# The reciprocal square roots of a hybrid backbone's norms: one power instruction on GpSimd in place of Newton steps on VectorE

## The chip, the core and the metric

The kernel runs on one core of a Trainium2 chip. The metric is the device time of one execution in microseconds (us). Before the change three runs gave 3520.69, 3523.40 and 3524.45 us, a median of 3523.4 us. A lower time is better.

## What is computed

Two layers of a diffusion backbone over 9 tiles of 128 tokens (8 latent, 1 context), 1024 features. Each layer norms, mixes and norms again; the mixers are grouped-query attention (GQA), low-rank attention (MLA) and a state-space part, with shared projections in and out and a squared-ReLU MLP behind.

```python
def rmsnorm(x, g):
    xf = x.astype(F32)
    y = xf * lax.rsqrt(jnp.mean(xf * xf, axis=-1, keepdims=True) + EPS)
    return (y * g.astype(F32)).astype(x.dtype)

def trunk_layer(x, mod, p, ctx):
    shift1, scale1, gate1, shift2, scale2, gate2 = jnp.split(mod[:, None, :].astype(x.dtype), 6, axis=-1)
    h = rmsnorm(x, p['norm_mix_pre']) * (1 + scale1) + shift1
    mix, ctx_tensors = token_mixers(h, p, ctx)
    x = x + gate1 * rmsnorm(mix, p['norm_mix_post'])
    h = rmsnorm(x, p['norm_ffn_pre']) * (1 + scale2) + shift2
    f = jnp.square(jax.nn.relu(h @ p['w_ffn1'])) @ p['w_ffn2']
    x = x + gate2 * rmsnorm(f, p['norm_ffn_post'])
    return x, ctx_tensors
```

Inside `token_mixers` there are more norms of the same kind: of each head of the queries and keys of GQA, of the compressed queries and keys of MLA, and of the output of the state-space part.

## The kernel before, in words

Tokens go in three blocks (b) of three tiles of 128. Every product is made of two float32r halves, high and low, so each weight is loaded (`raw`), its high half cast on ScalarE (line 65) and its low half subtracted on GpSimd (line 78, tile `w`, five buffers). GpSimd has this as its main work; it also does some adds of squares (`h`, `big`), rotary products (`rope_a`, `rope_b`) and parts of the state-space scan.

A layer goes through these stages: the in-projection (in the first layer up to about 395 us, in the second from about 1880 to 2140 us), the two attentions with the state-space outputs beside them (to 700 and 2440 us), the out-projection and the norms around it (to 960 and 2680 us), and the MLP in eight chunks, the last of which goes block by block with the closing norms beside it.

Every norm needs 1/sqrt of a few columns, made by `rsqrt` (lines 99 to 117) on VectorE: a first guess from the bits (`rs_i`, `rs_h`, `rs_r`, line 89), then three Newton steps of a product (line 83), a product (line 83) and a fused step (line 93). That is 12 instructions, or 9 where there is one column. It is called from four places:

- `stats` (line 274), three columns, 24 times: the norms over 1024 features. TensorE sums the squares (`st`), VectorE adds EPS (`st_v`), `rsqrt` follows, VectorE spreads the result over a diagonal, and TensorE broadcasts that (`rb`).
- `in_proj`, group 2 (line 632), two columns, 18 times: compressed queries and keys of MLA. ScalarE (`qcn`) and VectorE (`ckv`) scale the projection by it.
- `in_proj`, group 1 (line 664), eight columns, 18 times: heads of GQA. The tile's squares are summed on VectorE (`vv`, line 662), `rsqrt` follows, VectorE multiplies the projection `g` by it into `g_qn`, and the rotation follows on GpSimd and VectorE.
- `ssm_b` (line 1311), one column, 18 times: the state-space output (`yss`, `y`).

The order of instructions on each engine is not the order of the code. Work beside the main stream is issued by `pull`, which pays it against a credit that `spend` counts (lines 57 to 61); the Newton instructions go through `ts`, `tt` and `stt` and are counted there. Then the framework's scheduler orders each engine's instructions. The engines take their own in that order.

Of the kernel before, what the change touches and what calls it, by code (L numbers as in the profile page):

```python
# [13 lines left out]
L = 2  # L14
NT = 9            # token tiles: 8 latent, 1 context
NB = 3            # blocks of three token tiles
BK = 384
EPS = 1e-6
# how long (ns) background work is left alone where a chain over several engines is under way
# [3 lines left out]
# worth (ns) of background work issued at each point of the main stream  # L23
PU = (600, 850, 600, 500, 1100, 500, 400, 400, 500, 900)
SEG = [[(0, 384, 0)], [(0, 384, 0)], [(0, 256, 0), (256, 384, 1)]]
# columns of the packed small parameters
# [4 lines left out]
class Group:  # L31
    """One head of one block of queries in the attention stream."""
# [5 lines left out]
class Net:  # L38
# [7 lines left out]
    # ---------------------------------------------------------------- helpers  # L46
# [9 lines left out]
    # Rough prices (ns) of what is issued, so that background work can be paced.  # L56
# [42 lines left out]
    def rsqrt(self, v, n):  # L99
        """1/sqrt of v [128, n], by Newton's steps in float32."""  # L100
        sp, nc = self.sp, self.nc
        ii = sp.tile([128, 16], I32, name="rs_i", bufs=2)[:, :n]
        r = sp.tile([128, 16], F32, name="rs_r", bufs=4)[:, :n]
        h = sp.tile([128, 16], F32, name="rs_h", bufs=2)[:, :n]
        t = sp.tile([128, 16], F32, name="rs_t", bufs=2)[:, :n]
        self.ts(ii, v.bitcast(I32), 1, ALU.arith_shift_right)
        self.ts(r.bitcast(I32), ii, -1.0, ALU.mult, float(0x5F3759DF), ALU.add)
        self.ts(h, v, -0.5, ALU.mult)
        for _ in range(3):
            if n == 1:  # L110
                self.ts(t, r, r, ALU.mult, h, ALU.mult)
                self.ts(r, t, 1.5, ALU.add, r, ALU.mult)
            else:
                self.tt(t, r, r, ALU.mult)
                self.tt(t, t, h, ALU.mult)
                self.stt(r, t, 1.5, r, ALU.add, ALU.mult)
        return r
# [12 lines left out]
    # Work that runs beside the main stream: generators, advanced a step at a time.  # L130
    # One that yields a number is left alone for about so many ns.
# [7 lines left out]
    def turns(self, gens):  # L139
        """Advances the generators in the list in turn; more may be added to it meanwhile."""  # L140
        due = {}
        while gens:
            ready = [g for g in gens if due.get(g, 0) <= self.now]
            if not ready:
                g = min(gens, key=lambda g: due[g])
                yield due[g] - self.now
                ready = [g]
            for g in ready:
                try:
                    due[g] = self.now + (next(g) or 0)  # L150
                except StopIteration:
                    gens.remove(g)
                yield

    def pull(self, ns=500):
        """Issues background work worth ns of the engine that it uses most."""
        self.now += ns
        self.credit = min(self.credit + ns, ns)
        while self.bg and self.credit > 0 and self.now >= self.hold:
            u = list(self.used)  # L160
            self.hold = self.now + (self.step() or 0)
            self.credit -= max(MIN_STEP, *(b - a for a, b in zip(u, self.used)))
# [9 lines left out]
    # ------------------------------------------------------------- modulation  # L172
    def mods(self, l, groups, engs=None, raw=None, ps=None):
        """Columns of the modulation: at the start as products, later on VectorE, with a product
        that only sums over the partitions."""
        nc = self.nc
        sums = []
        for g in groups:
# [16 lines left out]
            elif l == 0 and g < 10:  # L195
                # four products of different k side by side in the array, 32 columns each, of which two count
# [59 lines left out]
    # ------------------------------------------------------------------ norms  # L256
# [3 lines left out]
    def squares(self, sq, src, h, dve=False, eng=None):  # L260
        """Squares of the h-th quarter of src, over 1024; their sum over the features of a partition
        is in sq[:, 0] after the last one."""
        hs = slice(2 * h, 2 * h + 2)
        if dve:
            self.stt(sq[:, hs], src[:, hs], 1.0 / 1024, src[:, hs], ALU.mult, ALU.mult)
        else:
            self.act(sq[:, hs], src[:, hs], AF.Square, scale=1.0 / 32)
        if h in (1, 2):
            self.tt(sq[:, 0:2], sq[:, 0:2], sq[:, hs], ALU.add, self.nc.gpsimd)
        if h == 3:  # L270
            self.tt(sq[:, 0:2], sq[:, 0:2], sq[:, hs], ALU.add, eng)
            self.tt(sq[:, 0], sq[:, 0], sq[:, 1], ALU.add, eng)

    def stats(self, sq, out, src=None, pool=None, tag="m", bufs=2):
        """Broadcast of rsqrt(mean(src^2) + eps) over features, [128, 384] in PSUM; without src,
        the squares are there."""
# [21 lines left out]
    def prenorm(self, l, which, x, b, hi, lo, sq, squared=False):  # L298
        """x (overwritten) -> modulated h, split in hi + lo; without sq, x is normed already."""
# [19 lines left out]
    def postnorm(self, l, which, src, x, b, sq, squared=False, again=False, lazy=False):  # L319
        """x += gate * gain * rmsnorm(src); src is overwritten. again: sq gets the squares of x.  # L320
        lazy: it isn't waited for, and GpSimd does what it can."""
# [28 lines left out]
    # ------------------------------------------------------------------ build  # L350
    def build(self):
# [6 lines left out]
        self.ident = self.cst[:, 0, :]  # L358
        self.small = []
# [8 lines left out]
        # silu of the conditioning, split  # L368
        # (what follows the conditions only keeps 32 columns in reach)
# [61 lines left out]
    # ---------------------------------------------------------------- in-proj  # L431
    def in_proj(self, l, hT):
# [54 lines left out]
        # ---- group 3: kpe | z | dt  # L487
# [12 lines left out]
        # ---- x, B, C of the state-space part: feature-major, with the convolution  # L500
# [27 lines left out]
        # the first two blocks before the last one, whose norm may still be under way  # L528
# [49 lines left out]
        # ---- group 2: va | qc | kvc, and the query up-projection of MLA  # L578
# [63 lines left out]
        # ---- group 1: qa | ka; its first products run ahead of what is left of group 2  # L642
# [38 lines left out]
    def rope(self, x, C, S, nh, q, tp, eng, eng2=None):  # L681
        """x [128, nh*d] in place: x*C + partner(x)*S, d = 4q."""
# [15 lines left out]
    def ssm_steps(self, l, b, tp):  # L698
        """Softplus of the steps of a block, cumulated decays; everything [128, dir, tile, head]."""
# [19 lines left out]
        # dA = -exp(a_log) * dt  # L719
# [35 lines left out]
    # -------------------------------------------------------------- attention  # L755
    def dup_split(self, pt, hi, lo, n):
        """pt rows (x; x): hi and lo in full."""
# [3 lines left out]
    def attn(self, groups, tp, ps):  # L761
        """Streams the groups: scores of the next one run beside the products with V of this one.
        A group has b, prep() -> pairs of (stationary [128, 384], moving [128, 1280]),
        V(j) -> [128 keys, (hi | lo)], scale, dst() and done()."""
# [8 lines left out]
        def score(g, i, j):  # L773
            """Scores of query tile i against the j-th third of the keys, with their maximum."""
# [93 lines left out]
    def qT(self, src, tp, ps, name):  # L868
        """src: three [128 tokens, 128] tiles -> split transposes."""
# [8 lines left out]
    # ------------------------------------------- the three mixers  # L878
    def mix(self, l):
        """MLA (beside it the state-space outputs, then keys and values of GQA), then GQA  # L880
        (beside it the out-projection of the blocks that are done)."""
# [9 lines left out]
        # ---- keys and values of MLA  # L891
# [72 lines left out]
        def query(src, h, n, rep, col):  # L964
            """Head h of the block at hand, n columns repeated rep times: [128, 3, rep * n]."""
# [122 lines left out]
    def ssm_a(self, l, ss):  # L1088
        """Per chunk: its state, and beside it the decayed scores (keys on the partitions)."""
# [18 lines left out]
        def front(t):  # L1108
            """The products of B and C of the chunk, both groups."""
# [32 lines left out]
    def ssm_inputs(self, l, t, cv, ss, out):  # L1142
        """Tokens of the chunk on the partitions: B, and x weighted for the chunk's end (start)."""
# [20 lines left out]
    def ssm_state(self, l, t, parts):  # L1164
        Sst = self.Sst
        bh, bl, xh, xl = parts
        if t < 7:
            # the forward state before the chunk, decayed over it (in a slot that is filled last)
# [20 lines left out]
    def ssm_scores(self, l, t, g, E, G, ss):  # L1189
# [4 lines left out]
        # the decay of a pair is the smaller of the two directions' (the other one's exponent is >= 0)  # L1194
# [18 lines left out]
    def ssm_rec(self, l, ss):  # L1213
        """The start states of the chunks: forward they are there, backward they are built here.
        The slots of the states that nothing follows hold the states given."""
# [12 lines left out]
    def ssm_b(self, l, ss):  # L1228
        """The outputs of the chunks, gated and normalised."""
# [173 lines left out]
    # -------------------------------------------------------------------- FFN  # L1403
    def ffn(self, l, h2):
# [61 lines left out]
        for c in range(7):  # L1466
# [3 lines left out]
            # the first chunk takes the last block by itself: its norm may still be under way  # L1470
# [28 lines left out]
        # the last chunk goes block by block: the norms of a block run beside the products of the next  # L1499
# [55 lines left out]
def lay(i):  # L1555
    """Layout of the inputs for the chip: reshapes, transposes, repeats."""
# [9 lines left out]
    def rows(w, n):   # [L, 1024, n] -> [L, 4, 128, 2n]  # L1566
# [67 lines left out]
```

## Time and profile before

| | |
|---|---|
| median of three runs | 3523.4 us |
| profiled execution, first to last instruction (span) | 3515.7 us |
| TensorE (PE) busy | 3229.9 us, 92% |
| VectorE (DVE) busy | 2400.3 us, 68%, 6199 instructions |
| ScalarE (ACT) busy | 1559.8 us, 44% |
| GpSimd (POOL) busy | 1279.6 us, 36%, 918 instructions |
| chain that ended last | PE 71%, DVE 20%, ACT 3%, DMA 3%, POOL 1% |

The profiled execution has no time of its own beside its span; the median is 7.7 us above that span. A share of busy time is an average over stages: TensorE is full through most of the two MLPs and has gaps in the in-projections and around the norms. The chain follows what was waited for last, back from the end; a piece of it on VectorE is time in which the next step waited for VectorE, or for its place in VectorE's queue.

### The profile page before, as it was taken

How to read it: one execution, taken by the hardware profiler on the slowest of the kernel's cores; microseconds unless marked ns; L12 is line 12 of the kernel's file. 1: busy time of each engine (PE TensorE's matmuls, PEld its weight loads, DVE VectorE, ACT ScalarE, POOL GpSimd, SP SyncE). 2: the span in 40 equal slices, each digit the busy share in tenths (PEclk: the TensorE clock that was granted, in tenths of full speed). 3: DMA queues.
4: the chain of work that ended last, by engine and by line, in shares of the span. 5: the costliest groups of instructions: out<-in, count | busy, mean ns of one | idle time of the engine just before them, and what ended most of it. 6: DMA issues, size and time to landing. Idle time of an engine off the chain costs nothing.

```text
span 3515.7 us, 51450 instructions
## 1 busy us (share of the span) xinstructions
PE 3229.9 (92%) x18578; PEld 3044.7 (87%) x18578; DVE 2400.3 (68%) x6199; ACT 1559.8 (44%) x3250; POOL 1279.6 (36%) x918
## 2 busy tenths in 40 slices
PE   6978799999799999999989778999887999999997
PEld 3966698788699999999989667989887999999997
DVE  7887898766666787784588878997758433333336
ACT  4454577766442211112444646787654412222223
POOL 5356432134651112112564553341446422222135
PEclk8989899999899999999999889999998999999998
DMA  5253323512322333332433533231223211111133
GB/s 205 80 172 108 113 72 107 184 49 96 125 93 82 96 96 98 95 91 78 139 120 102 169 105 108 81 98 61 80 98 103 79 49 42 43 43 43 40 105 132
DMA packets 164532, 340.77 MB, mean 97 GB/s; under 512 B 14429, under 2 KB 105909, under 8 KB 160693
## 3 DMA queue, kind: packets, MB, share of 16 engines
q1 hardware_dynamic: 161012, 335.32, 30.0%
q8 instruction: 146, 2.39, 0.3%
q10 hardware_dynamic: 3264, 2.16, 0.2%
q14 instruction: 110, 0.89, 0.1%
HBM read 280.99 MB, written 56.44 MB: 96 GB/s over the span
## 4 chain that ended last, share of the span: by engine, by line
PE 71%; DVE 20%; ACT 3%; DMA 3%; issue 2%; POOL 1%; SPq 0%; DVEq 0%; ACTq 0%; POOLq 0%
PE g L69 47%; PE S L69 5%; PE op L69 5%; PE oT L69 4%; PE pt L73 4%; DVE big L89 2%; PE m L69 2%; DVE rs_t L83 2%; PE m L73 2%; DVE cv L93 1%; DVE big L83 1%; DVE E L93 1%; DVE P L788 1%; DVE h L83 1%; DVE pl L78 1%
## 5 line engine op out<-in xcount | busy, mean ns | idle before, releaser
L78 POOL TENSOR_TENSOR w<-raw,w 128x1024 fp32r<-128x1024 f32 (+1 forms) x266 | 653.1, 2460 | 1409.3 <-ACT w L65 1365.8
L69 PE MATMUL g<-h,w 128*128 128x384 f32 x5328 | 953.6, 339 | 14.3 <-DVE h L78 12.9
L69 PEld LDWEIGHTS g<-h,w 128*128 128x128 f32 x5328 | 931.8, 189 | 17.7 <-DVE h L78 13.9
L69 PE MATMUL g<-big,w 128*128 128x384 f32 x4608 | 818.7, 336 | 13.7 <-DVE big L78 9.9
L69 PEld LDWEIGHTS g<-big,w 128*128 128x128 f32 x4608 | 800.6, 188 | 19.4 <-DVE big L78 12.0
L65 ACT CAST w<-raw 128x1024 fp32r<-128x1024 f32 (+1 forms) x266 | 275.9, 1041 | 651.6 <-PE g L69 366.1
L83 DVE TENSOR_TENSOR big<-big,g 128x384 f32<-128x384 f32 x336 | 182.9, 551 | 289.2 <-PE g L69 288.5
L83 DVE TENSOR_TENSOR r<-r 128x384 f32<-128x384 f32 x192 | 146.6, 765 | 294.3 <-ACT r L97 294.1
L69 PE MATMUL g<-w,h 128*128 128x512 f32 (+1 forms) x1296 | 320.9, 404 | 24.0 <-ACT w L65 6.1
L788 DVE TENSOR_SCALAR_CACHE_REDUCE P<-S 128x384 f32<-128x384 f32 (+1 forms) x500 | 265.9, 541 | 101.7 <-PE S L69 95.8
L69 PEld LDWEIGHTS g<-w,h 128*128 128x128 f32 x1296 | 255.7, 200 | 70.2 <-DVE h L78 6.9
L78 DVE TENSOR_TENSOR pl<-pt,ph 128x384 fp32r<-128x384 f32 (+2 forms) x560 | 270.2, 498 | 40.1 <-ACT ph L65 35.2
L65 ACT CAST ph<-pt 128x384 fp32r<-128x384 f32 (+2 forms) x560 | 233.1, 444 | 90.6 <-PE pt L73 77.6
L73 PE MATMUL pt<-cst,P 128*128 128x128 f32 x1460 | 256.1, 275 | 1.3 <-ACT P L97 0.9
L97 ACT ACTIVATE r<-g 128x384 f32<-128x384 f32 x192 | 94.3, 491 | 362.1 <-PE g L69 344.7
L93 DVE SCALAR_TENSOR_TENSOR macc<-raw,cT,macc 128x128 f32<-128x128 f32 x784 | 254.9, 389 | 0.0
L69 PE MATMUL op<-big,w 128*128 128x384 f32 x1152 | 227.1, 343 | 8.4 <-DVE big L78 8.4
L78 DVE TENSOR_TENSOR big<-r,big 128x384 fp32r<-128x384 f32 x192 | 167.7, 874 | 86.7 <-ACT big L65 86.3
L97 ACT ACTIVATE P<-P,mx 128x1152 f32<-128x1152 f32 x180 | 210.5, 1170 | 27.9 <-DVE mx L89 27.0
L69 PEld LDWEIGHTS op<-big,w 128*128 128x128 f32 x1152 | 202.8, 191 | 9.9 <-DVE big L78 9.0
L73 PEld LDWEIGHTS pt<-cst,P 128*128 128x128 f32 x1460 | 188.3, 142 | 16.8 <-issue 1.7
L65 ACT CAST big<-r 128x384 fp32r<-128x384 f32 x192 | 98.2, 512 | 185.4 <-DVE r L83 185.2
(299 smaller groups left out, 4933.9 us busy)
## 6 DMA issues: line engine op xcount, KB each, us to landing
raw<-in_w SPq DMA_DIRECT2D x176, 512.0 KB, 3.6
raw<-in_w_mod SPq DMA_DIRECT2D x80, 512.0 KB, 3.5
raw<-in_w_out SPq DMA_DIRECT2D x48, 512.0 KB, 3.6
big<-s_x SPq DMA_DIRECT2D x13, 1536.0 KB
E<-s_ac SPq DMA_DIRECT2D x36, 384.0 KB, 4.3
s_x<-big SPq DMA_DIRECT2D x9, 1536.0 KB
cv<-s_cv SPq DMA_DIRECT2D x36, 320.0 KB, 3.5
h<-in_w_mod SPq DMA_DIRECT2D x16, 512.0 KB, 9.2
```

The costliest lines, as they stand in the source:

```text
L65: self.nc.scalar.copy(out, in_)
L69: self.nc.tensor.matmul(out, lhsT=lhsT, rhs=rhs, start=start, stop=stop)
L73: self.nc.tensor.transpose(out, in_, self.ident[:p, :p])
L78: (eng or self.nc.vector).tensor_tensor(out=out, in0=src, in1=hi.bitcast(F32), op=ALU.subtract)
L83: (eng or self.nc.vector).tensor_tensor(out=out, in0=a, in1=b, op=op)
L89: (eng or self.nc.vector).tensor_scalar(out=out, in0=a, scalar1=s1, scalar2=s2, op0=op0, **kw)
L93: self.nc.vector.scalar_tensor_tensor(out=out, in0=a, scalar=s, in1=b, op0=op0, op1=op1)
L97: self.nc.scalar.activation(out=out, in_=in_, func=func, **kw)
L788: nc.vector.tensor_scalar(out=p[:, j * 384:j * 384 + nk], in0=S, scalar1=1.0, scalar2=None, op0=ALU.mult, op1=ALU.max, accum_out=mx[:, j:j ...
```

## The change

`rsqrt` keeps its callers and its result tile `rs_r`, and is now one `tensor_tensor` on GpSimd: `v` to the power of a constant tile of -0.5 (`half`, 128x16, filled once at the start). The instruction is issued without `spend`. Comments are dropped all through the file, which moves line numbers by 1 to 14; the new instruction is on line 102.

```diff
     def rsqrt(self, v, n):
-        """1/sqrt of v [128, n], by Newton's steps in float32."""
-        sp, nc = self.sp, self.nc
-        ii = sp.tile([128, 16], I32, name="rs_i", bufs=2)[:, :n]
-        r = sp.tile([128, 16], F32, name="rs_r", bufs=4)[:, :n]
-        h = sp.tile([128, 16], F32, name="rs_h", bufs=2)[:, :n]
-        t = sp.tile([128, 16], F32, name="rs_t", bufs=2)[:, :n]
-        self.ts(ii, v.bitcast(I32), 1, ALU.arith_shift_right)
-        self.ts(r.bitcast(I32), ii, -1.0, ALU.mult, float(0x5F3759DF), ALU.add)
-        self.ts(h, v, -0.5, ALU.mult)
-        for _ in range(3):
-            if n == 1:
-                self.ts(t, r, r, ALU.mult, h, ALU.mult)
-                self.ts(r, t, 1.5, ALU.add, r, ALU.mult)
-            else:
-                self.tt(t, r, r, ALU.mult)
-                self.tt(t, t, h, ALU.mult)
-                self.stt(r, t, 1.5, r, ALU.add, ALU.mult)
+
+        r = self.sp.tile([128, 16], F32, name="rs_r", bufs=4)[:, :n]
+        self.nc.gpsimd.tensor_tensor(out=r, in0=v, in1=self.half[:, :n], op=ALU.pow)
         return r
...
         self.ident = self.cst[:, 0, :]
+
+        self.half = per.tile([128, 16], F32, name="half")
+        nc.vector.memset(self.half, -0.5)
```

The order of the other instructions moves too, by the credit and by the scheduler. Two places show it.

VectorE near the end of the in-projection's group 1, first layer (`vv` sums of squares, `rs_` the root, `g_qn` the normed heads). Before:

```order
L662 TENSOR_REDUCE vv_3490<-g_qn 128x8
L93 SCALAR_TENSOR_TENSOR rs_r<-rs_t,rs_r 128x8
L89 TENSOR_SCALAR vv_3490<-vv_3490 128x8
L83 TENSOR_TENSOR rs_t<-rs_r 128x8
L89 TENSOR_SCALAR rs_i<-vv_3490 128x8
L89 TENSOR_SCALAR rs_h<-vv_3490 128x8
L83 TENSOR_TENSOR rs_t<-rs_t,rs_h 128x8
L89 TENSOR_SCALAR rs_r<-rs_i 128x8
L93 SCALAR_TENSOR_TENSOR rs_r<-rs_t,rs_r 128x8
```

The same place on VectorE with the change:

```order
L651 TENSOR_REDUCE vv_3180<-g_qn 128x8
L83 TENSOR_TENSOR g_qn<-g,rs_r 128x512
L89 TENSOR_SCALAR vv_3180<-vv_3180 128x8
L83 TENSOR_TENSOR rope_a<-g_qn,tabA 128x384
L83 TENSOR_TENSOR g_qn<-g,rs_r 128x512
L83 TENSOR_TENSOR g_qn<-rope_a,rope_b 128x384
L651 TENSOR_REDUCE vv_3226<-g_qn 128x8
```

Between one tile's sum and the next only the tile's own products are left on VectorE, and a tile's product by its root stands some rows behind its sum.

GpSimd at the close of the first layer's MLP, where the norm of the first block runs beside the products of the next (`w` low halves of weights, `h` and `big` squares and residual). Before:

```order
L83 TENSOR_TENSOR h<-h 128x768
L78 TENSOR_TENSOR w<-raw,w 128x1024
L83 TENSOR_TENSOR h<-h 128x768
L78 TENSOR_TENSOR w<-raw,w 128x1024 x4
L83 TENSOR_TENSOR big<-big 128x768
```

The same place on GpSimd with the change:

```order
L83 TENSOR_TENSOR h<-h 128x768
L78 TENSOR_TENSOR w<-raw,w 128x1024
L83 TENSOR_TENSOR h<-h 128x768
L78 TENSOR_TENSOR w<-raw,w 128x1024 x2
L102 TENSOR_TENSOR rs_r<-st_v,half 128x3
L78 TENSOR_TENSOR w<-raw,w 128x1024 x2
L83 TENSOR_TENSOR big<-big 128x768 x2
```

The power stands in GpSimd's queue behind two weight splits, and two more stand behind it.

## Rows read from the trace of the kernel before

**Rows 1.** Busy time by stretch: start:end, length, then each engine's busy us (instructions).

```profile
195.00:395.00 200.00, 151.39 (x661) 124.86 (x662) 163.05 (x505) 103.04 (x303) 111.78 (x162) 0.85 0.44 140
1720.00:1880.00 160.00, 143.53 (x779) 138.24 (x778) 136.85 (x245) 76.40 (x134) 97.74 (x43) 0.97 0.37 127
1880.00:2140.00 260.00, 206.27 (x926) 173.48 (x924) 221.07 (x582) 128.02 (x357) 135.09 (x172) 0.86 0.41 128
```

**Rows 2.** Chain by line: the whole span, then 195:395, 1720:1880 and 1880:2140.

```profile
by line: PE g L69 46.7%; PE S L69 5.1%; PE op L69 4.7%; PE oT L69 4.3%; PE pt L73 3.7%; issue 2.5%; DVE big L89 2.3%; PE m L69 2.1%; DVE rs_t L83 1.8%; PE m L73 1.6%; DVE cv L93 1.5%; DVE big L83 1.4%; DVE E L93 1.2%; DVE P L788 1.1%; DVE h
...
by line: PE g L69 22.6%; DVE rs_t L83 10.3%; DVE E L93 8.7%; DMA E<-s_ac 5.0%; issue 4.5%; DVE rs_r L93 4.1%; ACT E L97 3.9%; DVE g_qn L83 3.1%; PE m L69 3.0%; DMA raw<-in_w_in 2.2%; DVE vv L662 2.1%; DVE xw L83 2.0%; PE G L69 1.9%; DMA s_M
...
by line: PE g L69 38.0%; DVE big L83 11.6%; DVE rs_t L83 7.0%; issue 5.4%; DVE big L89 5.4%; DVE r L83 4.1%; DVE h L83 3.8%; POOL big L83 2.7%; POOL w L78 2.6%; DVE rs_i L89 2.5%; POOL h L83 2.4%; DVE big L78 2.3%; DVE rs_r L93 2.1%; DVE h 
...
by line: PE g L69 17.4%; DVE cv L93 12.5%; DVE E L93 9.1%; DVE rs_t L83 7.4%; issue 6.6%; DMA s_M<-E 3.0%; DMA s_qb<-qb 2.9%; DVE rs_r L93 2.8%; DVE g_qn L83 2.8%; DVE xw L83 2.1%; DVE vv L662 1.9%; DVE Gm L83 1.8%; DVE big L89 1.7%; DMA s_
```

**Rows 3.** VectorE's busy us with `rs_t` (195:395, then all) and with `rs_i` (all).

```profile
195.00:395.00 200.00, 45.60 (x162) 0.85 0.44 140
...
sum 3516.00, DVE 168.96; mean DVE 11.26
...
sum 3516.00, DVE 53.60; mean DVE 3.57
```

**Rows 4.** Timeline, in-projection group 2: start us, us, engine, line, operation.

```profile
275.11 7.09 POOL L78 TENSOR_TENSOR w<-raw,w 128x1024 fp32r<-128x1024 f32 x3 [5.94 <-ACT w L65]
275.23 2.34 DVE L83 TENSOR_TENSOR rs_t<-rs_t,rs_h 128x2 f32<-128x2 f32 x1
```

**Rows 5.** Timeline, end of the first in-projection: TensorE, VectorE and GpSimd.

```profile
359.35 10.43 PE L69 MATMUL g<-w,h 128*128 128x512 f32 x44
365.25 0.67 DVE L662 TENSOR_REDUCE vv<-g_qn 128x8 f32<-128x512 f32 x1
370.89 0.68 DVE L662 TENSOR_REDUCE vv<-g_qn 128x8 f32<-128x512 f32 x1
...
373.59 1.49 POOL L83 TENSOR_TENSOR rope_b<-g_qn,tabA 128x192 f32<-128x192 f32 x2 [0.92 <-DVE rs_t L83]
376.05 0.45 POOL L83 TENSOR_TENSOR rope_a<-g_qn,tabA 128x128 f32<-128x128 f32 x1 [0.97 <-DVE rs_t L83]
376.46 0.60 POOL L83 TENSOR_TENSOR rope_b<-g_qn,tabA 128x64 f32<-128x64 f32 x2
377.13 0.46 POOL L83 TENSOR_TENSOR g_qn<-rope_a,rope_b 128x128 f32<-128x128 f32 x1
...
389.23 3.20 PE L69 MATMUL k<-ckvT,wk 128*128 128x384 f32 x9 [2.81 <-ACT ckvT L65]
```

**Rows 6.** Timeline, VectorE: a root at the MLP's close, then the last root.

```profile
1729.16 1.90 DVE L89 TENSOR_SCALAR rs_i<-st_v 128x3 int32<-128x3 int32 x1
...
1735.80 0.16 DVE L93 SCALAR_TENSOR_TENSOR rs_r<-rs_t,rs_r 128x3 f32<-128x3 f32 x1
...
3499.75 0.17 DVE L89 TENSOR_SCALAR rs_i<-st_v 128x3 int32<-128x3 int32 x1
...
3501.73 0.16 DVE L93 SCALAR_TENSOR_TENSOR rs_r<-rs_t,rs_r 128x3 f32<-128x3 f32 x1
```

**Rows 7.** Groups of GpSimd by shape: operation, count, busy us, mean ns, idle before.

```profile
L78 POOL TENSOR_TENSOR w<-h,w 128x1024 fp32r<-128x1024 f32 x8 | 22.4, 2804 | 12.0 <-ACT w L65 10.6 <-DMA x<-in_xT 1.4
...
L83 POOL TENSOR_TENSOR rope_b<-qb,tabB 128x64 f32<-128x64 f32 x36 | 11.4, 337 | 0.0
...
L1625 POOL MEMSET const-float32-1.0<- 128x1 f32 x1 | 0.1, 98 | 0.0
```

**Rows 8.** Chain, a handover from VectorE to GpSimd: start us, us, piece.

```profile
384.43 0.70 DVE g_qn L83
385.30 1.49 POOL rope_b L83 x2
```

**Rows 9.** Waits of GpSimd: engine, line, released by: total us, times, longest us.

```profile
POOL w L78 <- ACT w L65: 1376.4, 172, 35.6
```

## The prediction

> **What bounds the kernel now.** The busy time by stretch comes first [rows 1]. In both in-projections and at the close of the first MLP no engine is full: TensorE works 151 of 200 us, 144 of 160 and 206 of 260, and VectorE 163, 137 and 221. So something is waited for in turns there, and the chain says what [rows 2]. In all of the span VectorE's `rs_t` is 1.8% of the chain, 63 us. In the first in-projection `rs_t` (10.3%) and `rs_r` on line 93 (4.1%) are 14.4% of 200 us, 28.8 us. In the second 7.4% and 2.8% of 260 us are 26.5 us. At the MLP's close 7.0%, 2.1% and `rs_i` with 2.5% are 11.6% of 160 us, 18.6 us. Those three hold 20.6 + 19.2 + 11.2 = 51 us of `rs_t`; the other 12 us lie elsewhere, in the first norms, the out-projections and the end. At the ratio of the first in-projection (28.8 to 20.6) that is 17 us of root. The roots hold some 91 us of the chain, and that is the most that their going can be worth directly.
>
> The next reading is why they cost so much. The 648 instructions with `rs_t` keep VectorE for 169 us and the 156 with `rs_i` for 54 [rows 3]. That is 0.26 us each for `rs_t`, while a step by itself takes 0.16 [rows 6]. The timeline shows the rest: a `rs_t` of two columns starts 0.12 us after GpSimd begins three weight splits and takes 2.34 us, one split's length [rows 4]. A step with two operands in SBUF stands still while GpSimd works. At the MLP's close the same happens to a root as a whole: it takes from 1729.16 to 1735.96, 6.8 us, against 2.14 us for the last one, with GpSimd idle beside it [rows 6].
>
> **The change part by part.** 882 instructions leave VectorE: 60 roots of 12 steps (24 with three columns, 18 with two, 18 with eight) and 18 of 9. 78 go to GpSimd. The memset of `half` lies at the start, where VectorE waits for the first loads: nothing. The rest has one unknown price.
>
> *What the power costs.* No row shows one. GpSimd's cheapest row, a memset of one column, takes 0.098 us; a product of 64 columns takes 0.337 us; the longest, 1024 columns, 2.804 us [rows 7]. Eight columns or fewer are nearest to the product of 64, whose time at that size is mostly fixed; a power does more per element than a product. I take 0.5 us and keep 0.1 and 2.8 for the range. A handover from VectorE to GpSimd is 385.30 - 385.13 = 0.17 us [rows 8], two of them 0.35. A root with nothing ahead of it in GpSimd's queue is then ready after 0.85 us, where 2.14 was the best before. 78 times 0.5 us is 39 us more on GpSimd, which is busy 112 of 200 us where the roots are thickest [rows 1]: it fits.
>
> *In-projection, last part.* TensorE's last product of group 1 ends at 359.35 + 10.43 = 369.8 us, and the next stage's `k` begins at 389.2 [rows 5]. Between them VectorE works off its backlog, one tile in 5.6 us (sums at 365.25 and 370.89), as fast as TensorE makes one: 24 products of 10.43/44 us, 5.7 us. Without the steps VectorE has per tile a sum, three products of half a us and a small add, about 3 us, and GpSimd 1.49 + 0.45 + 0.60 + 0.46 = 3.0 us plus the power, 3.5. Both are under TensorE's 5.7, so no backlog is left, and the stretch ends when the last tile is through: its sum 0.7 us, the power with handovers 0.85, the rotation's first two products on GpSimd 1.5 [rows 5], and, as an estimate, six more steps of half a us to 0.7 (the sum's length) on ScalarE and VectorE, 4 us. That is 7 us behind 369.8, at 377, 12 us earlier than 389.2. The second layer has the same stretch; I take 12 again.
>
> *In-projection, before that.* 28.8 - 12 = 17 and 26.5 - 12 = 14.5 us of chain are left. There the roots are mixed with the state-space scan, TensorE's products and loads, which were nearly as late: of VectorE's 163 us about 55 go (45.6 with `rs_t` [rows 3], and some 10 for the steps without it), and what is next in line is not far behind. I take half, 8 and 7 us. In sum 20 and 19 us.
>
> *Close of the first MLP.* 18.6 us, about four roots. The power waits for what GpSimd has in hand, a split of 2.4 us, by half on the average 1.2, so a root is 2.0 us: 8 us stay and 10 go. TensorE's gaps of 16 us in this stretch [rows 1] allow it.
>
> *Elsewhere.* 17 us of root; at 2.0 us for each of five or so, 10 stay or are caught by the next wait, and I count 7. The state-space norms (one column) run beside attention and are worth nothing.
>
> *What the power takes back.* It reads two operands on GpSimd and so stops VectorE's steps with two operands for its length, as the splits do: 39 us in all, of which a tenth on the path, 4 us. The order of other instructions moves as well; I price that at nothing, since it moves work within stretches that have gaps, and keep 10 us either way for the range.
>
> Sum: 20 + 19 + 10 + 7 - 4 = 52 us. The span goes from 3515.7 to 3463.7, and with the 7.7 us around it to **3471 us**.
>
> **The rivals.** *First: the standstill moves on.* The splits stay, and the next VectorE step with two operands waits in place of `rs_t`; the power holds VectorE too. Then only the steps' own time is won, 0.16 of 0.26, or 61%: 0.61 x 56 = 34 us, less 39 us of power of which a third would then be felt, 13 us: 21 us, **3502 us**. For it: a step of two columns is caught for a split's whole length [rows 4]. Against it: the in-projection's last part has no long split beside it [rows 5], and its 24 us do not hang on it. The Trainium skill, Perfetto Trace Analysis, section Optimizing Scalar/DVE Operations, goes further: since GpSimd and VectorE share an SBUF read port, moving work between the two might not help. By that alone nothing would be won, and the time would be 3523 us; the trace agrees on the sharing (2.34 us for a step of 0.16) and not on the size, as twelve instructions become one.
>
> *Second: the power is slow.* If its arithmetic runs lane by lane in software it can lie above every row of GpSimd. Per us, nine roots on the path (four and five, above) cost 9 us; and from the point at which GpSimd's tile, 3.0 us plus the power, passes TensorE's 5.7, at 2.7 us, the two last parts cost 18 us more. At 2.8 us that gives 3471 + 9 x 2.3 + 18 x 0.1 = 3494. The gain is used up where 9(p - 0.5) + 18(p - 2.7) = 52, at 3.9 us; at 5 us it is 3471 + 40 + 41 = **3552 us**, slower than before. For it: nothing in the trace excludes it. Against it: every row of GpSimd is a fixed part and some 2 ns a column.
>
> *Third: GpSimd's queue.* The power stands behind splits that wait for ScalarE's cast, 1376.4/172 = 8.0 us at a time, the longest 35.6 [rows 9]. If each of the nine roots on the path met one such wait, 72 us would come and the 17 us of the MLP's close and elsewhere go: 3471 + 17 + 72 = **3560 us**; it is level with before at 3.9 us of mean wait. Against it: at the close the splits come every few us, and the order puts the sums of squares, which the norm waited for already, in the same queue.
>
> *Fourth: no change.* TensorE's products are next in line everywhere, and all is hidden: 3523 us. Against it, its gaps [rows 1].
>
> **How the numbers follow.** My forecast has 0.62, the first rival 0.18, the slow power 0.09, the queue 0.06, no change 0.05. My own range runs from 3426 (all of the 91 us and 10 of order, where nine roots keep 0.45 us at a power of 0.1) to 3494 (the power at 2.8 us). The first rival ends at 3502, with 10 us of order and a smaller gain at 3512; to leave out no more than 2 in 10 the range goes from 3420 to 3525. About 0.2% (7 us) is what a measurement of this kernel can tell from no change. Faster by more than that: 0.62 and most of the first rival, 0.78. Within it: 0.07. Slower: the slow power and the queue, 0.15.
>
> **What would show it.** On GpSimd's list, 78 rows of `rs_r` at half a us. In the chain, no `rs_` on VectorE and at most 1% of the power. In the in-projections, VectorE near 105 of its stretch, and `k` some 8 us after the last product of group 1. At the MLP's close, a root ready within 3 us of `st_v`. I am wrong if the power is over 2.7 us, if GpSimd waits for a cast with a power behind it, or if other two-operand steps of VectorE grow by what `rs_t` lost.

## The result, and the profile after

| | before | after |
|---|---|---|
| median of four runs | 3522.05 us (3518.35 to 3524.45) | 3486.51 us (3478.20 to 3491.05) |
| ratio, 95% interval | 1 | 0.9900 (0.9887 to 0.9913) |
| span of the profiled execution | 3515.7 us | 3483.7 us |

The change makes the kernel 35.5 us faster by the medians, 32.0 by the spans. The forecast was 52 us faster, at 3471. The time lies in the range, and half way between the forecast and the first rival (3502). The profiled execution of after took 3485.52 us, 1.8 more than its span. So the 7.7 us that the prediction put around the span of before were mostly that execution's distance from the median. The stated range, 3420 to 3525, also holds the time of before, so that the result lies in it says little.

The page of the kernel after, its head and the busy times:

```profile
span 3483.7 us, 50649 instructions
...
PE 3234.2 (93%) x18578; PEld 3055.2 (88%) x18578; DVE 2257.0 (65%) x5318; ACT 1557.5 (45%) x3250; POOL 1348.8 (39%) x996
```

VectorE loses 881 instructions (882 and one memset) and 143 us, GpSimd gains 78 and 69 us. What each power costs stands in the list of groups by shape (operation, count, busy us and mean ns of one, idle time before):

```profile
L102 POOL TENSOR_TENSOR rs_r<-vv,half 128x8 f32<-128x8 f32 x18 | 31.1, 1727 | 6.2 <-DVE vv L89 6.2
...
L102 POOL TENSOR_TENSOR rs_r<-st_v,half 128x3 f32<-128x3 f32 x24 | 24.0, 998 | 57.1 <-DVE st_v L89 57.1
...
L102 POOL TENSOR_TENSOR rs_r<-vv,half 128x2 f32<-128x2 f32 x18 | 13.7, 763 | 15.1 <-DVE vv L89 14.9
...
L102 POOL TENSOR_TENSOR rs_r<-yss,half 128x1 f32<-128x1 f32 x18 | 9.9, 551 | 22.8 <-DVE yss L89 22.4
```

The power's price grows with the columns: 0.55 us for one, 1.73 for eight, some 0.17 us a column where a product costs a few ns [rows 7]. In sum it is 78.7 us, twice the 39 of the prediction. The queue, the third rival, cost little: the 78 powers began 0.5 us after their input on the average, at most 4.7.

Busy time in the stretches of [rows 1], after:

```profile
195.00:395.00 200.00, 162.41 (x723) 134.52 (x723) 135.54 (x297) 108.74 (x323) 130.49 (x178) 0.86 0.42 134
1720.00:1880.00 160.00, 142.60 (x743) 137.14 (x742) 139.95 (x194) 77.20 (x144) 99.79 (x47) 0.93 0.34 115
1880.00:2140.00 260.00, 211.61 (x1006) 180.92 (x1005) 190.74 (x391) 136.79 (x380) 155.39 (x197) 0.91 0.43 137
```

In the first stretch VectorE falls from 163 to 136 us, not to 105 as forecast, and GpSimd rises from 112 to 130: nearly as long as VectorE now. (The stretches are fixed in time, so by 1880 the kernel after is 13 us further on in its work.)

The chain of after can be followed back only to about 2030 us. So the stages are compared by landmarks on TensorE's timeline, the start of the same group of products in both kernels. The last line is the end of the span:

| landmark | before | after | moved by | gained in the stage |
|---|---|---|---|---|
| `k<-cst,kd`, first layer (start and in-projection) | 402.2 | 393.4 | -8.8 | 8.8 |
| `op` (attention) | 695.5 | 686.5 | -9.0 | 0.2 |
| second chunk's `g<-big` (out-projection, norms, MLP's start) | 1112.3 | 1096.9 | -15.4 | 6.4 |
| seventh chunk's `g<-big` (MLP) | 1637.3 | 1625.5 | -11.8 | -3.6 |
| first `g<-w,h`, second layer (MLP's close) | 1806.3 | 1793.2 | -13.1 | 1.3 |
| `k<-cst,kd`, second layer (in-projection) | 2155.3 | 2128.8 | -26.5 | 13.4 |
| `op` (attention) | 2421.4 | 2395.0 | -26.4 | -0.1 |
| first chunk's last `g<-h` (norms, MLP's start) | 2786.7 | 2753.7 | -33.0 | 6.6 |
| sixth chunk's last `g<-big` (MLP) | 3335.9 | 3308.8 | -27.1 | -5.9 |
| end (close) | 3515.7 | 3483.7 | -32.0 | 4.9 |

The sum of the last column is 32.0. Four things differ from the forecast: the in-projections gave 22.2 us and not 39, the first MLP's close 1.3 and not 10, the rest (norms behind the mixers, last close) 18 and not 7, and the two MLPs lost 9.5 us where the forecast had nothing. No root runs in those two rows, and TensorE's products themselves were slower there, as the last section shows for the second.

**The MLP's close.** GpSimd and VectorE around the second root of the first layer's close, timeline of after:

```profile
1743.11 3.11 POOL L78 TENSOR_TENSOR w<-raw,w 128x1024 fp32r<-128x1024 f32 x1
1746.17 2.16 POOL L83 TENSOR_TENSOR h<-h 128x768 f32<-128x768 f32 x1
1748.29 2.39 POOL L78 TENSOR_TENSOR w<-raw,w 128x1024 fp32r<-128x1024 f32 x1
1750.65 1.84 POOL L83 TENSOR_TENSOR h<-h 128x768 f32<-128x768 f32 x1
1752.46 1.17 POOL L102 TENSOR_TENSOR rs_r<-st_v,half 128x3 f32<-128x3 f32 x1
1753.61 7.70 POOL L78 TENSOR_TENSOR w<-raw,w 128x1024 fp32r<-128x1024 f32 x3
...
1747.62 0.16 DVE L89 TENSOR_SCALAR st_v<-st 128x3 f32<-128x3 f32 x1
...
1753.70 2.75 DVE L83 TENSOR_TENSOR h<-cst,rs_r 128x384 f32<-128x384 f32 x1
```

`st_v` is there at 1747.78. The power waits 4.7 us for two pieces of work ahead of it in GpSimd's queue, and is done 5.9 us after `st_v`. Then VectorE's next step, the spread over the diagonal, starts 0.09 us after a row of splits and takes 2.75 us. The kernel before had 0.56 for the same step, at 1736.00. So the standstill that `rs_t` had [rows 4] is now here. The Trainium skill, SBUF — State Buffer, SBUF: two separate sides, calls the pair of ports that GpSimd shares with VectorE an exclusive lock for a whole instruction; the trace agrees, with 2.75 us here where one split takes 7.70/3 = 2.57. Over the six roots of this close, the time from the end of `st_v` to the end of the root falls from 47.5 to 13.3 us, but the time from there to the broadcast that needs it (`rb`) only from 58.0 to 44.5. Over the whole span the standstill moved on in part: VectorE's instructions other than Newton's steps hold it for 2222.5 us before and 2257.0 after, 35 us more, where `rs_t` alone held it for 169 [rows 3].

**The end of the in-projection.** TensorE's `k` comes at 379.12 instead of 389.23 [rows 5]. GpSimd's last tile there, and the TensorE rows on both sides of the gap, after:

```profile
371.58 2.01 POOL L102 TENSOR_TENSOR rs_r<-vv,half 128x8 f32<-128x8 f32 x1 [0.59 <-DVE vv L89]
373.56 0.45 POOL L83 TENSOR_TENSOR rope_a<-g_qn,tabA 128x128 f32<-128x128 f32 x1
373.97 0.59 POOL L83 TENSOR_TENSOR rope_b<-g_qn,tabA 128x64 f32<-128x64 f32 x2
374.64 0.45 POOL L83 TENSOR_TENSOR g_qn<-rope_a,rope_b 128x128 f32<-128x128 f32 x1
375.17 1.51 POOL L83 TENSOR_TENSOR rope_b<-g_qn,tabA 128x192 f32<-128x192 f32 x2
377.35 0.45 POOL L83 TENSOR_TENSOR rope_a<-g_qn,tabA 128x128 f32<-128x128 f32 x1 [0.67 <-DVE g_qn L83]
377.76 0.60 POOL L83 TENSOR_TENSOR rope_b<-g_qn,tabA 128x64 f32<-128x64 f32 x2
378.44 0.45 POOL L83 TENSOR_TENSOR g_qn<-rope_a,rope_b 128x128 f32<-128x128 f32 x1
...
351.56 6.48 PE L69 MATMUL g<-w,h 128*128 128x512 f32 x27
379.12 10.79 PE L69 MATMUL k<-ckvT,wk 128*128 128x384 f32 x48 [9.18 <-ACT ckvT L65]
```

The products end at 358.04 and `k` starts 21.1 us later; it was 19.4 before, and 8 were forecast. During the nine rotations (327.1 to 378.9) GpSimd is busy for 40.0 of 51.8 us and VectorE for 33.1; in the kernel before it was 30.1 and 43.8 of 50.9. So the load has changed places, neither engine is full, and the tiles come no faster. One tile's rotation alone takes 375.17 to 378.89, 3.7 us with the wait for VectorE's sum in its middle; a power of 1.7 to 2.0 us for the next tile stands in the same queue.

### The profile page after: what moved, and what is told of

Read it like the earlier page. It is cut to its first block, busy times and chain, and to the rows that moved or that the text cites. A ratio compares the mean times of both kernels' runs of the same rounds, so it can differ in the third digit from the quotient of the medians.

```text
span 3483.7 us, 50649 instructions
## 1 busy us (share of the span) xinstructions
PE 3234.2 (93%) x18578; PEld 3055.2 (88%) x18578; DVE 2257.0 (65%) x5318; ACT 1557.5 (45%) x3250; POOL 1348.8 (39%) x996
## 5 line engine op out<-in xcount | busy, mean ns | idle before, releaser
L69 PE MATMUL g<-h,w 128*128 128x384 f32 x5328 | 971.5, 342 | 10.5 <-DVE h L78 6.4
L69 PEld LDWEIGHTS g<-h,w 128*128 128x128 f32 x5328 | 949.5, 190 | 16.5 <-DVE h L78 8.6
```

What stands on the lines that cost most here:

```text
L69: self.nc.tensor.matmul(out, lhsT=lhsT, rhs=rhs, start=start, stop=stop)
```

## The experiments

All twelve are variants of the two kernels. Those of the change that keep Newton's steps for some roots (e1 to e8, e12) have 8 columns instead of 16 in the small scratch tiles and in `half`. All were timed in five rounds beside the kernel before.

| run | median, us | ratio to before (95%) |
|---|---|---|
| after | 3486.5 | 0.9900 (0.9887 to 0.9913) |
| e1_stats: power for three columns only | 3483.2 | 0.9894 (0.9878 to 0.9910) |
| e2_proj2: for two columns only | 3503.4 | 0.9949 (0.9935 to 0.9963) |
| e3_heads: for eight columns only | 3518.6 | 0.9995 (0.9986 to 1.0005) |
| e4_ssm: for one column only | 3518.0 | 0.9998 (0.9988 to 1.0008) |
| e5_no_heads: for all but eight columns | 3473.3 | 0.9867 (0.9853 to 0.9881) |
| e6_mixer_ends: for 12 of the three-column roots | 3505.1 | 0.9957 (0.9944 to 0.9969) |
| e7_stats_dead: e1 and Newton's steps beside it | 3543.4 | 1.0062 (1.0050 to 1.0075) |
| e8_stats_charged: e1, counted in the pacing | 3498.9 | 0.9937 (0.9924 to 0.9951) |
| e9_before_unch: before, not counted | 3540.7 | 1.0069 (1.0056 to 1.0081) |
| e10_charged: after, counted | 3498.2 | 0.9940 (0.9927 to 0.9952) |
| e11_no_root8: after, no root for eight columns | 3461.1 | 0.9840 (0.9826 to 0.9853) |
| e12_no_heads_unch: e5, heads not counted | 3476.2 | 0.9878 (0.9863 to 0.9894) |

### One kind of root at a time

The four differ in one number, (3,), (2,), (8,) and (1,); Newton's steps follow as before for all other roots.

```diff
     def rsqrt(self, v, n):
+        if n in (3,):
+            r = self.sp.tile([128, 16], F32, name="rs_r", bufs=4)[:, :n]
+            self.nc.gpsimd.tensor_tensor(out=r, in0=v, in1=self.half[:, :n], op=ALU.pow)
+            return r
...
```

> The power only for the 24 roots of three columns (the norms over 1024 features, the close of the MLP among them); Newton's steps elsewhere. Theory A (the gain is Newton's steps taken out of VectorE's queue where a next step waits; the power's own price, 0.55 to 1.73 us by columns, eats some): TensorE's landmarks moved by 5.6 and 7 us at the mixers' ends and 1.3 us at the MLP's close, so 5 to 12 us faster than before. Rival B (the price of the power at the MLP's close is felt, because it stands behind weight splits, and that is why the close gave 1 us and not 10): no faster than 3 us, or slower. Rival C (the gain is the changed pacing, since the power isn't counted as work issued): the gain isn't bound to a kind of root, about 35.5 x 24/78 = 11 us here, and the same per root in the other three.

> The power only for the 18 roots of two columns (in-projection, group 2). A: these steps stood still beside weight splits (2.34 us for one of 0.16), so of the 22 us that the two in-projections gave together, 5 to 10 us. B: GpSimd has the splits in the same stretch, the power stands behind them, and what VectorE no longer waits is waited on GpSimd: 0 to 3 us. C: 35.5 x 18/78 = 8 us.

> The power only for the 18 roots of eight columns (in-projection, group 1). A: the end of the in-projection was VectorE's backlog (a tile in 5.6 us, of it more than 2 us of root), so 10 to 15 us faster than before, the larger part of the 22 us; the power is 1.73 us here and GpSimd's tile 4.7 us, under TensorE's 5.7. B: with 4.7 us for a tile, GpSimd's queue becomes the bound of the stretch: under 5 us. C: 35.5 x 18/78 = 8 us.

> The power only for the 18 roots of one column (state-space outputs, beside attention). A: attention kept its length from before to after, so within 4 us of before. B: as A. C: 35.5 x 18/78 = 8 us faster.

Measured, against 3519.5 us of before: 36, 16, 1 and 2 us faster. The norms over 1024 features alone give all that the full change gives, three times what A expected. Group 2 gives more than A had. The heads of GQA, from which A expected the most, give nothing, and the state-space roots nothing, as A and B said. Rival C's equal share for each root does not fit. The four together hold 55 us and the full change 35.5, 20 less; 9.5 of it is what the full change lost in the MLPs, where by their profiles these four lost 0.1 to 2.8 us each.

Where e1 gains most is behind the mixers: TensorE's `op` of the first layer stands 6.0 us earlier than before, the MLP's first `g<-big` 15.6. By the landmarks of the table 14.5 of its 31.6 us lie behind the two mixers, 11.5 in the start and the in-projections, and 4.0 in the two closes. In the kernel before VectorE interleaves a root with other work there, from 947.21 to 957.29, with one Newton step caught for 1.80 us:

```profile
945.05 0.15 DVE L89 TENSOR_SCALAR st_v<-st 128x3 f32<-128x3 f32 x1
...
947.21 0.16 DVE L89 TENSOR_SCALAR rs_i<-st_v 128x3 int32<-128x3 int32 x1
...
953.92 1.80 DVE L83 TENSOR_TENSOR rs_t<-rs_r 128x3 f32<-128x3 f32 x1
...
957.12 0.17 DVE L93 SCALAR_TENSOR_TENSOR rs_r<-rs_t,rs_r 128x3 f32<-128x3 f32 x1
```

That is 12.1 us behind `st_v`; in e1 the same root takes 1.2.

### The full change without the heads, and half of the norms

The condition of e1 becomes that of e5, and of e6, where `nroot` counts the roots of three columns:

```diff
-        if n in (3,):
+        if n in (1, 2, 3):
```

```diff
-        if n in (3,):
+        self.nroot = getattr(self, "nroot", -1) + (n == 3)
+        if n == 3 and self.nroot in (3, 4, 5, 6, 7, 8, 15, 16, 17, 18, 19, 20):
```

> The power for one, two and three columns, Newton's steps for the 18 roots of eight columns (heads of GQA). The four kinds alone gave 36, 16, 1 and 2 us, in sum 55, and all together 35.5. Theory A2 (the heads' power, 1.73 us, takes the place of VectorE's steps in a chain from tile to tile over GpSimd and VectorE and gives nothing, while its 31 us on GpSimd and the stops it makes take back some of the gain of the others): without it 3470 to 3478 us, some 10 us faster than the full change. Rival S (the gains of the norms and of group 2 overlap: what one gives is waited for elsewhere): 3483 to 3488 us, as the full change. Rival H (the heads' power helps once the others are gone): slower than the full change, 3490 us or more.

> The power only for the 12 roots at the two mixers' ends (the third to the eighth and the fifteenth to the twentieth of the 24 with three columns, counted from 0); Newton's steps for all else. The run with all 24 moved TensorE's start of the MLP by 13 us against the out-projection's start in the first layer and by 15 in the second. Theory A (the gain is bound to the place): 20 to 28 us faster than before, and the other 12 roots, at the start and the closes, hold the remaining 8 to 16. Rival M (the first MLP takes back what comes before it, and what counts is the close of the MLP, where the roots went from 47 us to 14 in sum): 10 to 16 us faster.

e5 has 3473.3 us, 13 less than the full change, inside what A2 gave; H falls. **By its median it is the fastest of the variants with the whole computation**, faster than both kernels. But A2's reason is not shown by it. Between the profiled spans of after and e5 lie 13.8 us, and by the landmarks 8.0 of them are in the two MLPs (2.1 and 5.9), where no root of the heads runs and e5 has the quicker products of before; the two in-projections differ by 1.3. So the heads' power took back a few us at most, and an overlap of the gains, as S has it, is not excluded: the three kinds of e5 hold 54 us one by one and 47 together.

e6 is 15 us faster, as rival M had it and not A: the 12 roots behind the mixers hold somewhat under half of the 36, the other 12, by difference, the rest. M's reason is not borne out: in e1 the first MLP's close gave 0.7 us.

### VectorE's time, or the wait for the root

The twelve steps stand where they stood and write a scratch tile (`rs_d`); what is returned is the power:

```diff
+        if n == 3:
+            p = sp.tile([128, 16], F32, name="rs_r", bufs=4)[:, :n]
+            nc.gpsimd.tensor_tensor(out=p, in0=v, in1=self.half[:, :n], op=ALU.pow)
...
-        return r
+        return p if n == 3 else r
```

> As the run with the power for three columns, but VectorE also goes through the twelve Newton steps of each of these 24 roots, on a scratch tile that nothing reads (work added, no result changed by it). Theory L (what counts is how long the next step waits for its root: twelve steps in a chain that VectorE does between its other work): the gain stays, 25 to 36 us faster than before. Rival V (what counts is VectorE's time, and the steps that stand still beside GpSimd): the gain goes, within 8 us of before, as the steps are still in VectorE's queue.

The gain is gone and 23 us more: theory L falls. The roots come as early as in e1 (43 us for the 24 against 41, from `st_v` to the root; 170 before), but the spread behind them waits in VectorE's queue. From `st_v` to TensorE's broadcast the 24 take 164 us, against 210 before and 130 in e1: the wait is shorter than before, and the kernel slower. So the gain is VectorE's time and its queue, not the earlier root. The dead steps are counted in the pacing as Newton's steps are in before, so the fair pair is e8 below, 3498.9 us, 45 less. Rival V said within 8 us of before. The profiled spans of e7 and before differ by 26.8 us: 26.5 lie behind the two mixers and 7.4 in slower products of the MLPs (last section), and other stages give some of it back. Why the place behind the mixers loses so much isn't explained by any one wait of its profile.

### The pacing

The change issues the power without `spend`, so background work is paid out as if the roots cost nothing. In e8 (three columns) and e10 (all; one column with its own nine steps) the price is put back:

```diff
+            for i in range(3):
+                self.spend(2, v, 0.6, 68)
+            for _ in range(3):
+                self.spend(2, v, 1.04, 68)
+                self.spend(2, v, 1.04, 68)
+                self.spend(2, v, 1.2, 68)
```

In e9 and e12 it is taken from Newton's steps, by a line ahead of them and one behind:

```diff
+        used = list(self.used)
         self.ts(ii, v.bitcast(I32), 1, ALU.arith_shift_right)
...
+        self.used = used
         return r
```

> As the run with the power for three columns, but each root is counted as the Newton steps were when background work is paced. Theory A: pacing is nothing, within 5 us of that run, 3478 to 3488 us. Rival C (the gain is the changed pacing): at least half of the 36 us goes, 3500 us or more.

> The kernel before, with all its Newton steps on VectorE, but none of them counted when background work is paced. No instruction is added or left out; only the order of the work changes. Charging the 24 norm roots cost 16 us of their 36. Theory P (the pacing is worth that by itself): 3500 to 3510 us, 10 to 20 us faster than before. Rival Q (the freer pacing only pays where VectorE has the room that the power leaves): within 5 us of before, or slower.

> The full change, each root counted as the Newton steps were. Theory P: of its 35.5 us some 10 to 20 go, 3495 to 3505 us. Rival (with all kinds of root changed the order is another, and the credit of one root is nothing): 3482 to 3491 us.

> The best version so far (the power for one, two and three columns, Newton's steps for the heads), with the heads' steps not counted either. Theory P: the credit of 18 roots, 0.85 us each, lies in the in-projections alone, where work is issued in turns: 0 to 6 us faster than 3473. Rival: the order of the in-projections is spoilt, 3476 us or more.

Counting the roots costs 16 us of the 36 in e1 (3498.9, just under the 3500 that C needed; A falls) and, by medians and by ratios, 12 to 14 of the 35.5 in the full change, as P had it. But the pacing isn't worth anything by itself: in the kernel before, the freer pacing costs 23 us (P falls, and Q holds with its "or slower"); 17.4 of them lie behind the two mixers. For the heads alone it does nothing that the intervals separate (0.9878 against 0.9867). So pacing and power are not two terms that add: the freer order pays only where VectorE has room.

The place is seen behind the first mixer. VectorE in e1, from the second block's `st_v` to its spread:

```profile
914.19 0.15 DVE L89 TENSOR_SCALAR st_v<-st 128x3 f32<-128x3 f32 x1
914.26 6.47 DVE L89 TENSOR_SCALAR big<-big,der 128x256 f32<-128x256 f32 x12
920.65 0.15 DVE L89 TENSOR_SCALAR st_v<-st 128x3 f32<-128x3 f32 x1
920.72 0.54 DVE L83 TENSOR_TENSOR h<-cst,rs_r 128x384 f32<-128x384 f32 x1
```

and in e8, with TensorE's broadcast that waits for it:

```profile
913.12 0.15 DVE L89 TENSOR_SCALAR st_v<-st 128x3 f32<-128x3 f32 x1
913.19 14.28 DVE L89 TENSOR_SCALAR big<-big,der 128x256 f32<-128x256 f32 x12
927.39 0.55 DVE L83 TENSOR_TENSOR h<-cst,rs_r 128x384 f32<-128x384 f32 x1
...
928.08 1.62 PE L69 MATMUL rb<-h,cst 128*128 128x384 f32 x2 [12.76 <-DVE h L83]
```

The root is there in 3 us in both. Ahead of the spread stands the same row of twelve steps, 6.47 us in one and 14.28 in the other, and TensorE waits 12.8 us for it in e8. Beside it GpSimd works without a pause from 907.0 to 926.9 us in e8: weight splits, the power and a product, in another order than in e1, where it stands idle for 1.61 us ahead of its second power. That this order is why the row of steps takes 14.28 us is argued from these two places, not tested.

### What the heads' root is worth

```diff
-            r = self.rsqrt(vv, 8)
+            r = vv
```

> The full change without any root in the heads' norm (the eight columns of sums are used as they are; the computation leaves out those 18 roots). It bounds what they can be worth. The full change has 3486 us, Newton's steps for the heads alone 3473. Theory K (the tiles go one after the other through the rotation on GpSimd and VectorE, about 5 us each with or without a root, and the power's 31 us on GpSimd are added to that): 3465 to 3475 us, about as with Newton's steps. Rival (the heads' root is on the path in either form): 3455 us or less. Rival (the power of the heads costs nothing, and what differs is only the order): 3480 us or more.

3461.1 us, between what the theory and its first rival gave: 25 us faster than the full change (3486.5) and 12 faster than with Newton's steps (3473.3). So the heads' root is on the path in either form. That the power costs twice what Newton's steps cost doesn't follow: e11 has the slower products of after in its MLPs, and e5 hasn't. By the landmarks the start and the two in-projections are 25.0 us shorter in e11 than in after, and 23.7 shorter than in e5; the root costs about as much in either form, as e3 measured it (1 us). K was wrong to give a tile the same time with and without a root. From the first `rope_b` of group 1 to the last `g_qn` on GpSimd, nine tiles take:

| | first layer, us | second layer, us |
|---|---|---|
| before | 338.1 to 389.0: 50.9 | 2093.9 to 2141.0: 47.1 |
| e3_heads | 336.7 to 383.5: 46.8 | 2096.1 to 2141.9: 45.8 |
| after | 327.1 to 378.9: 51.8 | 2062.4 to 2115.4: 53.0 |
| e5_no_heads | 324.8 to 374.5: 49.7 | 2055.5 to 2106.8: 51.3 |
| e11_no_root8 | 325.0 to 366.6: 41.6 | 2048.5 to 2090.9: 42.4 |

The full change has 10.2 and 10.6 us more than e11 here, 20.8 of the 25. Two tiles of e11 on GpSimd, without a power between them:

```profile
361.23 0.46 POOL L83 TENSOR_TENSOR rope_a<-g_qn,tabA 128x128 f32<-128x128 f32 x1 [2.35 <-DVE g_qn L83]
361.64 0.60 POOL L83 TENSOR_TENSOR rope_b<-g_qn,tabA 128x64 f32<-128x64 f32 x2
362.31 0.46 POOL L83 TENSOR_TENSOR g_qn<-rope_a,rope_b 128x128 f32<-128x128 f32 x1
362.88 1.49 POOL L83 TENSOR_TENSOR rope_b<-g_qn,tabA 128x192 f32<-128x192 f32 x2
365.05 0.45 POOL L83 TENSOR_TENSOR rope_a<-g_qn,tabA 128x128 f32<-128x128 f32 x1 [0.67 <-DVE g_qn L83]
365.46 0.60 POOL L83 TENSOR_TENSOR rope_b<-g_qn,tabA 128x64 f32<-128x64 f32 x2
366.13 0.45 POOL L83 TENSOR_TENSOR g_qn<-rope_a,rope_b 128x128 f32<-128x128 f32 x1
```

A rotation takes 3.7 us, from 362.88 to 366.58, and the power's 1.73 is laid on it, tile by tile: 18 of them are 31 us. Between after and e5 only 2.1 and 1.7 us of their 13 lie here. Most of the rest are the 8.0 us in the MLPs, of which the last section tells.

## Why the prediction was right and wrong

**Right:** the sign, and the reason: VectorE was in the way where its small steps stand still beside GpSimd (e7: with the steps back on VectorE nothing of the gain is left). It said so of steps with two operands; in its own rows a step with one, `rs_i`, took 1.90 us where another takes 0.17 [rows 6]. The state-space roots gave nothing (e4). That the sum came within 17 us of the result is partly luck: the in-projections and the close were put 26 us too high, the rest 11 too low, and the pacing and the MLPs' products were not in it.

**The power's price** was taken at 0.5 us, from the nearest row, a product of 64 columns. It is 0.55 to 1.73 us. The argument that the time of few columns is "mostly fixed" was wrong for eight: on some 0.4 us that do not depend on the columns come 0.17 for each (an estimate from the four rows). The price stayed under the 2.7 us at which the prediction let the second rival begin, but that limit was too high. It took GpSimd's tile as 3.0 us; e11's nine tiles come every 4.6 us without a power, which leaves 1.1 us to TensorE's 5.7, and the power of eight columns is over that.

**In-projection, last part: 12 + 12 us.** This step failed. It said that without Newton's steps both engines' tiles are under TensorE's 5.7 us and the backlog goes. The nine rotations took 51.8 and 53.0 us after, 50.9 and 47.1 before: the part gave nothing (e3: 4 and 1 us). It added up GpSimd's work per tile but left out the wait for VectorE in the middle of a rotation, and undersized the power. A tile took 51.8/9 = 5.8 us, no less than TensorE's 5.7, and TensorE had made the first tiles already when the rotations began (in the kernel after 128 of its 216 products), so that head start was never worked off.

**In-projection, before that: 8 + 7 us.** Undersized. The first rotation starts 11.0 us earlier (338.1 to 327.1), some of which the norms at the start gave, and 31.5 in the second layer, of which 13.1 were there at its start: 18.4. The roots of two columns alone, by e2, are worth 16 us in sum. The in-projections as a whole gave 22.2 and not 39.

**Close of the first MLP: 10 us.** Gave 1.3. The power's wait in GpSimd's queue was taken as half a split, 1.2 us; it was up to 4.7. And the next step of VectorE, the spread, took over the standstill: rival one, in this place.

**Elsewhere: 7 us.** Gave some 18, behind both mixers (13) and in the last close (4.9). The chain by line showed only 12 us of `rs_t` there [rows 2], and the rest of a root's time behind the mixers stood under the names of the work that VectorE did between its steps (`big`, `h`). From `st_v` to the root it took 3.8 to 12.1 us there, at six of the twelve 7 or more, and not its share of `rs_t`.

**Not in the sum:** the pacing. The order of other instructions was priced at nothing with 10 us either way; it is 12 to 14 us of the 35.5 (e10), and by itself, without the power, it would have cost 23 (e9). No row of before named its place. Nor were the MLPs' slower products in it, 9.5 us the other way.

## What to carry to other kernels

A chain by line puts a small interleaved sequence at its own instructions only; before pricing its removal, take the time from the sequence's input to its consumer at each place. Work moved to an engine that stands in the same loop gains nothing there: the 18 roots of the heads gave 1 us by themselves. Before a difference between two variants is put down to what was changed, compare the stages that the change does not touch: 8 of the 13.8 us between after and e5 lay in such a stage. Where a scheduler paces by declared costs, a new instruction without a cost is a second change, and it is measured apart.

## What was not expected of the hardware

The power on GpSimd costs by the column: 551, 763, 998 and 1727 ns for 1, 2, 3 and 8 columns of 128 partitions (L102 above), where a difference of 1024 columns takes 2.8 us [rows 7].

TensorE did the same products of the second MLP in 549.2 us in the profile of before and in 555.0 in that of after, at the same granted clock. Busy time by stretch, first after, then before:

```profile
2754.00:3309.00 555.00, 555.00 (x3170) 555.00 (x3169) 169.75 (x262) 116.71 (x187) 105.74 (x44) 1.00 0.15 42
```

```profile
2786.70:3335.90 549.20, 549.20 (x3171) 549.20 (x3169) 170.13 (x262) 116.70 (x187) 106.06 (x44) 1.00 0.15 43
```

TensorE is busy throughout and the granted clock is 1.00 in both. The difference lies in one kind of product. The 288 products `g<-h,w` of one chunk, after, then before:

```profile
2955.40:3006.20 50.80, 50.80 (x289) 50.80 (x289) 15.09 (x23) 15.15 (x26) 8.01 (x4) 1.00 0.11 32
```

```profile
2986.40:3036.30 49.90, 49.90 (x290) 49.90 (x289) 15.13 (x23) 15.14 (x26) 8.07 (x4) 1.00 0.12 33
```

In after every second one of them is followed by the next after 177 to 180 ns, and the others after 174 to 176; in before all but two after 173 or 174. The `g<-big,w` products of the same chunks take 49.8 us in both. Each full chunk of the second MLP repeats it, and so do the profiles of e10 and e11; in e7 two of every five are slow, and in the other nine variants, as in before, none. So it goes with the kernel and not with one execution. In the first MLP single slow steps stand in every profile, so its 3.6 us are not wholly this. After, e10 and e11 are the kernels without the scratch tiles of Newton's steps, e7 has one tile more than e1, and these small tiles are allocated ahead of the weights' tiles. Whether the place of a tile in SBUF is the reason, no run tests.
